# A two-layer hybrid decoder trunk: pre-norm row factors applied at the ends of the products, and the attention bias read from one small DRAM copy

## The chip, the cores and the metric

The kernel runs on one core of one Trainium2 chip. The time is device microseconds (us) of one execution. TensorE (PE) multiplies, VectorE (DVE), ScalarE (ACT) and GpSimd (POOL) do the rest, SyncE (SP) issues the loads of the weights. PE writes into PSUM; DVE and ACT read PSUM and SBUF. Each engine takes its instructions in the order of its own queue, and waits on semaphores where a value comes from another engine or from a DMA.

## The reference

The input `x` has 256 tokens (rows) of 1024 channels, in float32. There are two layers, each with FFN1, a mixer and FFN2; the mixer of layer 0 is an RG-LRU block, that of layer 1 is attention with one shared K and V, computed from the stream after layer 0.

```
def rms_norm(x, g):
    y = x * lax.rsqrt(jnp.mean(x * x, axis=-1, keepdims=True) + RMS_EPS)
    return y * g
def macaron_ffn(x, pre_g, post_g, w_gate, w_up, w_down):
    h = (silu(n @ w_gate) * (n @ w_up)) @ w_down          # n = rms_norm(x, pre_g)
    return x + 0.5 * rms_norm(h, post_g)
# layer:  x = macaron_ffn(x, ...); x = x + rms_norm(mixer(rms_norm(x, mix_pre_g)), mix_post_g)
#         x = macaron_ffn(x, ...)
# after layer 0:  k, v = split(rms_norm(x, kv_norm_g) @ w_kv)
# attention, one block of 256 keys:
#   s = q @ k.T * scale + rel_bias[h, t5_bucket(t - j)], -inf where j > t;  softmax(s) @ v
```

A pre-norm is thus a factor per row (token), `r = 1/sqrt(mean(x*x) + eps)`, and a gain per channel.

## The kernel before

Tokens lie in two tiles of 128 (`tt` 0 and 1), `x[tt]` stays in SBUF. Every float32 operand of a product is split into a high and a low float32r part, and a product is three PE products (`mm3`, L267 to L270): high by high, high by low, low by high. A weight piece of 2048 columns by 128 rows is loaded by SP into `raw`, and four instructions of ACT (`whi`, L273 or, with a channel's gain, L277) and four of DVE (`wlo`, L274 or L278) split it; three `raw` buffers and five pairs of `whi` and `wlo` are in flight. All weights, some 176 MB, pass through once.

Between two stages stands a **boundary**. When a token tile's last product has ended, `post` (L304) squares and sums it (ACT, `junk`), works out the post-norm's row factor (POOL, L288 and L289), and adds it to `x` (DVE, L313, two halves). Then `normed` (L317) does the same for the next stage's pre-norm: two squares on ACT, two sums on POOL, and `x` times the factor into `kb` (ACT L324 and DVE L325, half each). Then `turned` (L327) transposes `kb` on PE in eight 128x128 blocks (L336) and splits the result into `big`, the left or moving operand of the next stage. While tile 0 goes through this, PE still does products of tile 1; how many are left for it at that point is set in the code by where `turn_now` stands.

In the FFN the first four channel chunks are done token by token (`by_token`: gate and up for 128 tokens, `x` as the weights of PE); the later units channel by channel (`by_channel`, `wide`), where the result has channels on partitions and tokens along the free dimension. `dn` are the down products into `acc`. RG-LRU uses `yproj`, `yproj3` (by token), `xproj`, `yproj4` (by channel), `gates` and `scan`; attention uses `vals` (by token), `key` and `query` (by channel).

The attention bias: in FFN2 of layer 0 `bias_rows` makes 8 rows of 384 numbers, `bias_out` (L806) writes every row 128 times to DRAM, 8 x 128 x 384 x 4 bytes, in one DMA issued on ACT's queue, and in FFN1 of layer 1 `bias_tables` (L810) reads two tables of 128 x 4 x 256 back, with a step of 383 between partitions, so that each query row sees its row shifted by one.

The order of instructions on each engine is set when the kernel is built, by the order in the code with the weight splits at a lower priority (`Prog`).

Of the kernel before, what the change touches and what calls it, by code (L numbers as in the profile page):

```python
# [38 lines left out]
KB1 = 6  # L39
KB2 = 19  # L40
# [3 lines left out]
WIDE = True  # L44
# [42 lines left out]
def trunk_kernel(ctx, tc, t, out):  # L87
# [46 lines left out]
    make_identity(nc, ident)  # L134
    mhalf = cp.tile([P, 1], F32, tag="mhalf", name="mhalf")
# [149 lines left out]
    def rstd(ss, f):  # L285

        m, r = small(), small()
        nc.gpsimd.tensor_scalar(m, ss[:, 0:1], ss[:, 1:2], f * f * EPS, op0=ALU.add, op1=ALU.add)  # L288
        nc.gpsimd.tensor_tensor(r, m, mhalf, op=ALU.pow)  # L289
        return r  # L290
# [13 lines left out]
    def post(tt, src, g, half, out_rows=None):  # L304
# [6 lines left out]
        r = rstd(ss, f)  # L311
        for sl, y in zip(HALVES, ys):
            nc.vector.scalar_tensor_tensor(x[tt][:, sl], y, r, x[tt][:, sl], op0=ALU.mult, op1=ALU.add)  # L313
            if out_rows is not None:
                nc.sync.dma_start(out_rows[:, sl], x[tt][:, sl])

    def normed(tt, state):  # L317

        ss = small(2)
        for n, a in enumerate(halves(x[tt])):  # L320
            square_sum(a, 1.0, ss[:, n:n + 1])
        r = rstd(ss, 1.0)
# [4 lines left out]
    def turned(tt, state, g=None):  # L327
# [25 lines left out]
    def between(state, g, half=True):  # L353
# [12 lines left out]
    def ffn(which, l, state, after, nxt, middle={}, first=None):  # L366
# [40 lines left out]
        def by_channel(n):  # L407
# [3 lines left out]
            def wide(gi):  # L411
# [15 lines left out]
                if gi == 1:  # L427
# [8 lines left out]
            def go(gi):  # L436
                if WIDE:
                    return wide(gi)
                if gi == 0:
                    st["b", n] = bank().rearrange("p (g s) -> p g s", g=2)  # L440
                b = st["b", n]
                for k in range(KD):
                    wv = [a.rearrange("p (k g f) -> p k g f", k=4, g=2)[:, k % 4, gi, ft * P:(ft + 1) * P]
                          for a in pieces[keys(c)[k // 4]]]
                    mm3(b[:, gi, :], wv, xT(state, k), k == 0, k == KD - 1)
                if gi == 1:
                    sl, hd = kb1(), kb1()
                    nc.scalar.activation(sl, b[:, 0, :], AF.Silu)
                    nc.vector.tensor_mul(hd, b[:, 1, :], sl)
                    h = kb2(F32R, (P, 2, S))  # L450
                    split(h[:, 0, :], h[:, 1, :], hd)
                    for tt in range(NT):
                        hT[n, tt] = [h[:, part, tt * P:(tt + 1) * P] for part in range(2)]
            for gi in range(2):
                prog.add(lambda gi=gi: go(gi), *keys(c))
# [13 lines left out]

        def finish(units):  # L470
# [11 lines left out]
            prog.add(lambda: after(0, oacc[0], st["g"]))  # L482
# [9 lines left out]
            prog.add(lambda: after(1, oacc[1], st["g"]))  # L492

        if first is not None:
# [5 lines left out]
            tr(0, 0)  # L500
            by_channel(2)
# [29 lines left out]
        tr(1, 1)  # L531
        dn(3, 0)
# [35 lines left out]
    def recurrent(l, state, after, nxt):  # L568
# [10 lines left out]
        def yproj(tt, khs=(0, 1)):  # L579

            def use(b):
                st["sb", tt] = kb2()
                nc.scalar.activation(st["sb", tt], b, AF.Copy)
            by_token("lru_w_in", l, 2, tt, state, None, use, khs)

        def yproj3(tt):
# [3 lines left out]
            def go():  # L590
                b = bank()[:, 0:S]
                w = [a.rearrange("p (k f) -> p k f", k=8) for a in pieces[key]]
                for k in range(KD):
                    mm3(b, xT(state, k, tt), [a[:, k, :] for a in w], k == 0, k == KD - 1)
                st["sb3", tt] = kb1()
                nc.scalar.activation(st["sb3", tt], b, AF.Copy)
# [9 lines left out]
        def yproj4(n):  # L606

            def use(b):
                st["y4", n] = b
# [31 lines left out]
        def xproj(h, n):  # L641

            def use(b):
# [4 lines left out]
                nc.scalar.activation(cv[:, n, :], b, AF.Identity, scale=wcol[3], bias=cbias[:, 0, k:k + 1])  # L648
                for w in (2, 1, 0):
                    back = CW - 1 - w  # L650
                    nc.vector.scalar_tensor_tensor(cv[:, n, back:], b[:, 0:S - back], wcol[w],
# [97 lines left out]
        yproj3(1)  # L749
        xproj(0, 0)  # L750
# [42 lines left out]
    skew = {}  # L793

    def bias_rows():
# [6 lines left out]
        rr = skew["rows"] = big(shape=(P, Y))  # L802
# [3 lines left out]
    def bias_out():  # L806
        skew["dram"] = dp.tile([NH, P, Y], F32, tag="skew", name="skew")
        nc.scalar.dma_start(skew["dram"], skew["rows"][:NH, 0:Y].unsqueeze(1).to_broadcast([NH, P, Y]))

    def bias_tables():  # L810
        d = skew["dram"]
# [7 lines left out]
    def attention(j, l, state, kv_state, after, nxt):  # L819
# [7 lines left out]
        def vals(c, tt, khs=(0, 1)):  # L827
            def use(b):
                st["v", c, tt] = kb2()
                nc.scalar.activation(st["v", c, tt], b, AF.Copy)  # L830
            by_token("w_kv", None, 2 + c, tt, kv_state, ("kv_norm_g", 0), use, khs)

        def keep(what, h):
            def use(b):
                a = st[what, h] = kb2(F32R, (P, 2, S))
                split(a[:, 0, :], a[:, 1, :], b)
            return use

        def key(h):
            by_channel("w_kv", None, h // 2, h % 2, kv_state, ("kv_norm_g", 0), keep("k", h))  # L840
# [26 lines left out]
        def turned_p(h):  # L867
            def go():
# [3 lines left out]
                nc.tensor.transpose(pt[:, 0:P], p0[:, 0:P], ident)  # L872
                nc.tensor.transpose(pt[:, P:2 * P], p1[:, 0:P], ident)
                nc.tensor.transpose(pt[:, 2 * P:3 * P], p1[:, P:2 * P], ident)
# [100 lines left out]
    def begin():  # L975
        load_rows("first", (("ffn1_pre_g", 16),))
        normed(0, s1)
        turned(0, s1)
    begin()

    def second():
        load_x(1)
        with tc.issue_after(first_split[3].ins):
            normed(1, s1)
        s1["turn", 1] = lambda: turned(1, s1)
# [7 lines left out]
    def last(tt, src, g):  # L993
        post(tt, src, g, True, out.rearrange("b s d -> (b s) d")[tt * P:(tt + 1) * P, :])
# [3 lines left out]
    ffn(1, 1, s4, between(s5, ("mix_pre_g", 1)), s5, {9: bias_tables})  # L998
# [51 lines left out]
```

## Time and profile before

| | |
|---|---|
| median of 3 runs | 980.27 us (979.67 to 980.37) |
| the profiled execution | 980.36 us, span 978.5 us |
| PE busy | 943.1 us, 96% of the span |
| DVE, ACT, POOL busy | 69%, 64%, 3% |
| read from DRAM | 175.76 MB, 182 GB/s over the span with what is written |

The span goes from the first to the last instruction on the core. PE's busy time is modelled, and a busy PE need not be at its peak; idle time is what the trace shows between two of its instructions, with the event that ended it.

### The profile page before, as it was taken

Reading aid. Unit: us, or ns where it says so; the run is one execution under the profiler, and the core shown is the slowest. Engines: PE = TensorE matmul, PEld = TensorE weight load, DVE = VectorE, ACT = ScalarE, POOL = GpSimd, SP = SyncE. Lnnn points to the kernel's source line nnn. Section 1 sums busy time; section 2 is a strip of 40 time slices with the busy share of each in tenths; the row PEclk is TensorE's granted clock in tenths of the full one; section 3 lists DMA queues with packets and bytes.
Section 4 is the critical chain, followed back from the end, with each engine's and each line's share of the span. In section 5 each row is a group of like instructions: output and inputs, shape, how many; then the busy total and the mean of one; then the engine's idle time right before and its main releaser. Section 6 shows DMA issues by size and latency. Waiting matters only on the chain.

```text
span 978.5 us, 14039 instructions
## 1 busy us (share of the span) xinstructions
PE 943.1 (96%) x5124; PEld 808.6 (83%) x5124; DVE 675.5 (69%) x1332; ACT 631.1 (64%) x1325; POOL 26.8 (3%) x55
## 2 busy tenths in 40 slices
PE   6999999999989999599999999999999999999997
PEld 5888888879967888488878888887999878888886
DVE  5867775787888655385776767567987776757563
ACT  7757665678987655275775656567875675656562
POOL 1000000010010000000010000001000010000000
PEclk9999999999999999889999999999999999999999
DMA  8955656555157665676556656654735346656621
GB/s 258 327 170 186 202 188 221 166 175 194 49 171 261 201 207 118 162 231 200 160 187 235 208 179 192 196 193 153 236 130 176 126 129 237 203 185 184 203 86 44
DMA packets 131774, 179.29 MB, mean 183 GB/s; under 512 B 4689, under 2 KB 113401, under 8 KB 131705
## 3 DMA queue, kind: packets, MB, share of 16 engines
q1 hardware_dynamic: 129040, 175.65, 55.5%
q10 hardware_dynamic: 2664, 2.74, 1.9%
q8 instruction: 40, 0.66, 0.3%
q14 instruction: 30, 0.24, 0.1%
HBM read 175.76 MB, written 2.62 MB: 182 GB/s over the span
## 4 chain that ended last, share of the span: by engine, by line
issue 49%; PE 46%; POOL 2%; ACT 2%; DMA 1%; DVE 0%; SPq 0%; POOLq 0%; DVEq 0%; ACTq 0%
PE bank L421 7%; PE trb L421 7%; PE acc L268 4%; PE acc L269 4%; PE acc L270 4%; PE bank L268 3%; PE bank L269 3%; PE bank L270 3%; PE bank L420 3%; PE trb L420 3%; POOL small L288 1%; POOL small L289 1%; ACT junk L283 1%; DMA raw<-in_ffn_w_up_dram 1%; PE trb L423 0%
## 5 line engine op out<-in xcount | busy, mean ns | idle before, releaser
L278 DVE SCALAR_TENSOR_TENSOR wlo<-raw,cols,whi 128x512 fp32r<-128x512 f32 (+1 forms) x400 | 271.3, 726 | 66.2 <-ACT whi L277 66.1
L277 ACT ACTIVATE whi<-raw,cols 128x512 fp32r<-128x512 f32 (+1 forms) x400 | 255.9, 697 | 56.4 <-PE acc L270 27.3
L421 PE MATMUL bank<-big,whi 128*128 128x512 f32 x592 | 215.3, 398 | 0.0
L421 PE MATMUL trb<-big,whi 128*128 128x512 f32 x592 | 212.7, 394 | 0.0
L274 DVE TENSOR_TENSOR wlo<-raw,whi 128x512 fp32r<-128x512 f32 x264 | 170.7, 687 | 47.1 <-ACT whi L273 46.5
L268 PE MATMUL acc<-whi,kb 128*128 128x512 f32 x384 | 152.3, 397 | 10.4 <-ACT kb L273 10.4
L273 ACT ACTIVATE whi<-raw 128x512 fp32r<-128x512 f32 x264 | 151.0, 622 | 17.1 <-PE bank L269 8.2
L269 PE MATMUL acc<-wlo,kb 128*128 128x512 f32 x384 | 150.6, 392 | 0.0
L270 PE MATMUL acc<-whi,kb 128*128 128x512 f32 x384 | 149.7, 392 | 0.0
L420 PE MATMUL bank<-big,wlo 128*128 128x256 f32 x518 | 145.6, 281 | 0.0
L420 PE MATMUL trb<-big,wlo 128*128 128x256 f32 x518 | 143.4, 277 | 0.0
L421 PEld LDWEIGHTS bank<-big,whi 128*128 128x128 f32 x592 | 111.3, 188 | 23.6
L421 PEld LDWEIGHTS trb<-big,whi 128*128 128x128 f32 x592 | 111.0, 187 | 19.4
L420 PEld LDWEIGHTS bank<-big,wlo 128*128 128x128 f32 x518 | 98.1, 189 | 3.0
L420 PEld LDWEIGHTS trb<-big,wlo 128*128 128x128 f32 x518 | 97.3, 188 | 3.5
L268 PEld LDWEIGHTS acc<-whi,kb 128*128 128x128 f32 x384 | 72.6, 189 | 24.1 <-ACT kb L273 11.5
L270 PEld LDWEIGHTS acc<-whi,kb 128*128 128x128 f32 x384 | 72.6, 189 | 15.7
L269 PEld LDWEIGHTS acc<-wlo,kb 128*128 128x128 f32 x384 | 72.7, 189 | 14.9
L426 DVE TENSOR_TENSOR kb<-kb,trb 128x256 f32<-128x256 f32 x74 | 30.9, 418 | 76.1 <-ACT kb L425 76.0
L425 ACT ACTIVATE kb<-bank 128x256 f32<-128x256 f32 x74 | 28.5, 385 | 79.1 <-PE bank L421 79.1
L268 PE MATMUL bank<-whi,big 128*128 128x512 f32 (+1 forms) x176 | 70.4, 402 | 2.1 <-ACT big L273 1.4
L269 PE MATMUL bank<-wlo,big 128*128 128x512 f32 (+1 forms) x176 | 68.6, 393 | 0.0
(165 smaller groups left out, 1257.0 us busy)
## 6 DMA issues: line engine op xcount, KB each, us to landing
raw<-in_ffn_w_gate_dram SPq DMA_DIRECT2D x88, 512.0 KB, 4.1
raw<-in_ffn_w_up_dram SPq DMA_DIRECT2D x88, 512.0 KB, 5.1
raw<-in_ffn_w_down_dram SPq DMA_DIRECT2D x44, 1024.0 KB, 5.0
raw<-in_lru_w_in_dram SPq DMA_DIRECT2D x8, 1024.0 KB, 5.4
raw<-in_w_kv_dram SPq DMA_DIRECT2D x8, 1024.0 KB, 5.1
raw<-in_lru_w_out_dram SPq DMA_DIRECT2D x4, 1024.0 KB, 5.0
raw<-in_attn_w_q_dram SPq DMA_DIRECT2D x4, 1024.0 KB, 5.3
raw<-in_attn_w_o_dram SPq DMA_DIRECT2D x4, 1024.0 KB, 4.9
```

What stands on the lines that cost most here:

```text
L268: nc.tensor.matmul(o, a[0], b[0], start=start, stop=False)
L269: nc.tensor.matmul(o, a[0], b[1], start=False, stop=False)
L270: nc.tensor.matmul(o, a[1], b[0], start=False, stop=stop)
L273: nc.scalar.activation(hi, src, AF.Copy)
L274: nc.vector.tensor_sub(lo, src, hi.bitcast(F32))
L277: first_split.append(nc.scalar.activation(hi, src, AF.Copy, scale=g))
L278: nc.vector.scalar_tensor_tensor(lo, src, g, hi.bitcast(F32), op0=ALU.mult, op1=ALU.subtract)
L283: nc.scalar.activation(junk, a, AF.Square, scale=f / 32.0, accum_out=ss)
L420: nc.tensor.matmul(b[:, 1, :], wv[1], xt[:, 0, :], start=False, stop=False)
L421: nc.tensor.matmul(b, wv[0], xt, start=k == 0, stop=k == KD - 1)
L425: nc.scalar.activation(y, b[:, 1, :], AF.Copy)
L426: nc.vector.tensor_add(y, y, b[:, 0, :])
```

## The change

Row factors. Where a product's result has tokens on partitions, ACT's copy or Silu out of PSUM takes the factor as its scale; where it has tokens along the free dimension, DVE multiplies by a tile `R` of 128 x 256 that holds the factors of all tokens in every partition, made by `spread` once per stage. `turned` then transposes `x` itself; `factors` comes behind it. In an FFN only the gate is multiplied: the missing factor of the up product goes through to the post-norm, which removes it, with an epsilon made for it on POOL. The attention's queries keep the old way (`normed`), and are transposed by `flip`, a reversed identity, so that query rows run backwards and a bias table can be read with a step of 1 between partitions from one row per head.

```
-KB1 = 6
-KB2 = 19
+KB1 = 7
+KB2 = 17
+    flip = cp.tile([P, P], F32, tag="flip", name="flip")
...
+    def factors(tt, state):
+        ss = small(2)
+        for n, a in enumerate(halves(x[tt])):
+            square_sum(a, 1.0, ss[:, n:n + 1])
+        m = row("mean")
+        state["r", tt] = rstd(ss, EPS, m, row("factor"))
+        state["eps", tt] = row("eps")
+        nc.gpsimd.tensor_scalar(state["eps", tt], m, 4.0 * EPS, None, op0=ALU.mult)
+
+    def spread(state):
+        def go():
+            state["R"] = ws.tile([P, S], F32, tag="spread", name=nm("spread"), bufs=2)
+            pt = trb()
+            for tt in range(NT):
+                nc.tensor.transpose(pt[:, tt * P:(tt + 1) * P], state["r", tt].to_broadcast([P, P]), ident)
+            nc.vector.tensor_copy(state["R"], pt[:, 0:S])
+        prog.add(go)
...
+        src = state["xn", tt] if ("xn", tt) in state else halves(x[tt])
...
-                nc.tensor.transpose(pt[:, k * P:(k + 1) * P], state["xn", tt][h][:, k * P:(k + 1) * P], ident)
+                nc.tensor.transpose(pt[:, k * P:(k + 1) * P], src[h][:, k * P:(k + 1) * P],
+                                    ident if turn is None else turn)
...
-        def after(tt, src, post_g):
-            post(tt, src, post_g, half)
-            normed(tt, state)
-            state["turn", tt] = lambda: turned(tt, state, g)
+        def after(tt, src, post_g, eps=None):
+            post(tt, src, post_g, half, eps)
+            if turn is not None:
+                normed(tt, state)
+            def go():
+                turned(tt, state, g, turn)
+                if turn is None:
+                    factors(tt, state)
+            state["turn", tt] = go
...
-                        nc.scalar.activation(sl, b[:, 0:FC], AF.Silu)
+                        nc.scalar.activation(sl, b[:, 0:FC], AF.Silu, scale=state["r", tt])
...
+                if gi == 0:
+                    nc.vector.tensor_mul(y, y, state["R"])
+                else:
...
-                nc.scalar.activation(cv[:, n, :], b, AF.Identity, scale=wcol[3], bias=cbias[:, 0, k:k + 1])
+                xb = kb1()
+                nc.vector.tensor_mul(xb, b, state["R"])
+                nc.scalar.activation(cv[:, n, :], xb, AF.Identity, scale=wcol[3], bias=cbias[:, 0, k:k + 1])
...
-        skew["dram"] = dp.tile([NH, P, Y], F32, tag="skew", name="skew")
-        nc.scalar.dma_start(skew["dram"], skew["rows"][:NH, 0:Y].unsqueeze(1).to_broadcast([NH, P, Y]))
+        bias["dram"] = dp.tile([NH, Y], F32, tag="bias", name="bias")
+        nc.scalar.dma_start(bias["dram"], bias["rows"][:NH, 0:Y])
...
-            src = bass.AP(tensor=d.tensor, offset=d.offset + 127 + 4 * q * P * Y,
-                          ap=[[Y - 1, P], [P * Y, 4], [1, S]])
+            src = bass.AP(tensor=d.tensor, offset=d.offset + 4 * q * Y, ap=[[1, P], [Y, 4], [1, S]])
...
-                nc.tensor.transpose(pt[:, 0:P], p0[:, 0:P], ident)
+                nc.tensor.transpose(pt[:, 0:P], p0[:, 0:P], flip)
```

`yproj4` and `key` get the same multiplication by `R` as `xproj`; `yproj`, `yproj3` and `vals` get the factor as the scale of their copies. Over the whole program DVE gains 92 multiplications of 128x256 (74 in the FFNs, 10 in RG-LRU, 8 keys) and 5 copies of `spread`, and loses 10 of its 12 L325; ACT loses 10 of its 12 L324; PE gains 10 transposes; POOL gains 10 small products for the epsilons.

The order on PE where RG-LRU hands over to FFN2 of layer 0. `acc` with the higher number is the second half of tile 1's output product, `trb` takes the transposes, and `bank` is FFN2's first product. Before:

```order
L268 MATMUL acc_2798<-whi_2813,big_2793 128x512
L269 MATMUL acc_2798<-wlo_2814,big_2793 128x512
L270 MATMUL acc_2798<-whi_2813,big_2793 128x512
L336 MATMUL trb_2926<-ident,kb_405_2888 128x128 x4
L336 MATMUL trb_2935<-ident,kb_406_2889 128x128 x4
L268 MATMUL bank_2995<-whi_2838,big_2922 128x512
```

The same place on PE in the changed kernel:

```order
L366 MATMUL trb_2960<-ident,x_67 128x128 x4
L366 MATMUL trb_2969<-ident,x_67 128x128 x4
L272 MATMUL acc_2844<-whi_2860,big_2840 128x512
L273 MATMUL acc_2844<-wlo_2861,big_2840 128x512
L274 MATMUL acc_2844<-whi_2860,big_2840 128x512
L272 MATMUL acc_2845<-whi_2860,big_2840 128x512
L273 MATMUL acc_2845<-wlo_2861,big_2840 128x512
L274 MATMUL acc_2845<-whi_2860,big_2840 128x512
L272 MATMUL bank_3027<-whi_2885,big_2956 128x512
```

The transposes of tile 0 read `x` and stand ahead of the last six products of tile 1's output, not behind them.

The order on DVE at that place in the changed kernel, from tile 1's output (`acc_2844`, `acc_2845`) on. `big` are the splits of tile 0, `x_165` is tile 1 of the stream, and `wlo_3018` is the low part of the second weight piece of FFN2:

```order
L771 TENSOR_TENSOR kb_422_2995<-acc_2844,bout_1977 128x512
L771 TENSOR_TENSOR kb_423_2996<-acc_2845,bout_1977 128x512
L278 TENSOR_TENSOR big_2957<-trb_2960,big_2957 128x2x128
L278 TENSOR_TENSOR big_2958<-trb_2969,big_2958 128x2x128
L315 TENSOR_TENSOR kb_425_3000<-kb_422_2995,gain_1975 128x512
L315 TENSOR_TENSOR kb_426_3001<-kb_423_2996,gain_1975 128x512
L278 TENSOR_TENSOR big_2959<-trb_2969,big_2959 128x2x128
L318 SCALAR_TENSOR_TENSOR x_165<-kb_425_3000,small_3009,x_165 128x512
L318 SCALAR_TENSOR_TENSOR x_165<-kb_426_3001,small_3009,x_165 128x512
L282 SCALAR_TENSOR_TENSOR wlo_3018<-raw_3014,cols_904,whi_3017 128x512 x2
```

Both updates of tile 1's `x` stand ahead of the second weight piece's low part, as they do in the kernel before (`x_162` ahead of `wlo_2986`); the multiplication of tile 0 (L325) is gone.

## Rows read from the trace of the kernel before

**Rows 1.** PE's waits over the span: for whom, total, times, longest.

```profile
PE acc L268 <- ACT kb L273: 10.4, 1, 10.4
PE trb L336 <- ACT kb L324: 10.2, 7, 2.8
```

**Rows 2.** Windows: length, busy PE, PEld, DVE, ACT, POOL, granted clock, DMA share, GB/s.

```profile
405.50:416.00 10.50, 0.13 (x1) 0.13 (x1) 3.98 (x8) 4.00 (x9) 0.00 (x0) 0.62 0.78 234
416.00:422.00 6.00, 6.00 (x16) 4.74 (x17) 4.81 (x9) 4.97 (x11) 0.00 (x0) 0.52 0.79 242
288.80:292.00 3.20, 3.18 (x8) 2.50 (x9) 2.35 (x6) 2.83 (x7) 1.07 (x2) 0.50 0.51 177
```

**Rows 3.** Timeline of ACT in FFN2 of layer 0: start, length, [idle before, releaser].

```profile
373.15 0.79 ACTq L808 DMA_DIRECT2D skew<-big  x1
...
410.75 1.33 ACT L277 ACTIVATE whi<-raw,cols 128x512 fp32r<-128x512 f32 x2 [15.67 <-DMA raw<-in_ffn_w_up_dram]
```

**Rows 4.** DMA view, 383 to 393 us in 40 slices; then issues, KB, us to landing.

```profile
DMA  4444444444444444446364454545554877699998
GB/s 49 49 43 49 49 49 49 49 49 49 49 49 49 49 49 70 109 135 147 100 164 119 152 158 129 158 125 152 174 180 164 207 225 188 182 258 256 238 233 184
...
gain<-in_ffn_post_g_dram SPq DMA_DIRECT2D x4, 512.0 KB, 6.5
...
big<-skew ACTq DMA_DIRECT2D x2, 512.0 KB, 3.7
```

**Rows 5.** Timeline of PE: the transposes at the boundaries and their waits.

```profile
198.17 1.09 PE L336 MATMUL trb<-ident,kb 128*128 128x128 f32 x8 [1.24 <-ACT kb L324]
...
287.33 1.09 PE L336 MATMUL trb<-ident,kb 128*128 128x128 f32 x8 [2.81 <-ACT kb L324]
...
296.60 0.55 PE L336 MATMUL trb<-ident,kb 128*128 128x128 f32 x3 [0.48 <-ACT kb L324]
...
492.35 1.09 PE L336 MATMUL trb<-ident,kb 128*128 128x128 f32 x8 [1.42 <-ACT kb L324]
...
784.82 1.09 PE L336 MATMUL trb<-ident,kb 128*128 128x128 f32 x8 [0.72 <-ACT kb L324]
```

**Rows 6.** Timeline where RG-LRU hands over to FFN2.

```profile
282.31 1.42 DVE L313 SCALAR_TENSOR_TENSOR x<-kb,small,x 128x512 f32<-128x512 f32 x2 [0.84 <-POOL small L289]
...
286.56 0.72 ACT L324 ACTIVATE kb<-x,small 128x512 f32<-128x512 f32 x1 [0.53 <-POOL small L289]
...
286.96 1.28 DVE L740 TENSOR_TENSOR kb<-acc,bout 128x512 f32<-128x512 f32 x2
...
292.00 0.74 DVE L313 SCALAR_TENSOR_TENSOR x<-kb,small,x 128x512 f32<-128x512 f32 x1
...
292.66 0.75 DVE L278 SCALAR_TENSOR_TENSOR wlo<-raw,cols,whi 128x512 fp32r<-128x512 f32 x1
...
294.46 0.50 PE L269 MATMUL bank<-wlo,big 128*128 128x512 f32 x1
```

**Rows 7.** Timeline of the start, ACT and PE.

```profile
8.65 1.33 ACT L277 ACTIVATE whi<-raw,cols 128x512 fp32r<-128x512 f32 x2 [1.00 <-DMA raw<-in_ffn_w_up_dram]
...
10.30 0.80 PE L268 MATMUL bank<-whi,big 128*128 128x512 f32 x1 [0.63 <-ACT big L273]
```

**Rows 8.** Groups by form: count, busy us, mean ns, idle before.

```profile
L426 DVE TENSOR_TENSOR kb<-kb,bank 128x256 f32<-128x256 f32 x74 | 31.0, 418 | 41.3 <-ACT kb L425 41.2
...
L325 DVE TENSOR_SCALAR kb<-x,small 128x512 f32<-128x512 f32 x12 | 5.8, 486 | 12.9 <-POOL small L289 12.9
```

**Rows 9.** Windows in RG-LRU and at the start of attention, columns as in rows 2.

```profile
250.00:275.00 25.00, 24.33 (x150) 21.27 (x149) 24.15 (x43) 24.27 (x44) 0.00 (x0) 1.00 0.26 85
...
675.00:700.00 25.00, 23.76 (x142) 20.79 (x141) 23.06 (x52) 22.89 (x61) 3.48 (x7) 1.00 0.60 196
```

**Rows 10.** Timeline of ACT in one channel unit of FFN2.

```profile
369.57 0.42 ACT L429 ACTIVATE kb<-kb 128x256 f32<-128x256 f32 x1 [0.61 <-DVE kb L426]
...
371.49 0.36 ACT L425 ACTIVATE kb<-trb 128x256 f32<-128x256 f32 x1
```

More of the change, by code (lines that the diff above doesn't have):

```diff
@@ L134, in trunk_kernel @@
     make_identity(nc, ident)
+    flip = cp.tile([P, P], F32, tag="flip", name="flip")
+    nc.gpsimd.memset(flip, 0.0)
+    nc.gpsimd.affine_select(out=flip, in_=flip, pattern=[[1, P]], compare_op=ALU.not_equal, fill=1.0,
+                            base=-(P - 1), channel_multiplier=1)
     mhalf = cp.tile([P, 1], F32, tag="mhalf", name="mhalf")
@@ L310, in post @@
             nc.vector.tensor_mul(ys[n], src[n], g[:, HALVES[n]])
-        r = rstd(ss, f)
+        r = rstd(ss, f * f * EPS if eps is None else eps)
         for sl, y in zip(HALVES, ys):
@@ L325, in normed, with row, turned @@
         nc.vector.tensor_scalar(state["xn", tt][1], x[tt][:, HALVES[1]], r, None, op0=ALU.mult)
-    def turned(tt, state, g=None):
+    def row(tag):
+        return ws.tile([P, 1], F32, tag=tag, name=nm(tag), bufs=6)
+    def factors(tt, state):
[14 more added lines that the diff above has]
+        prog.add(go)
+    def turned(tt, state, g=None, turn=None):
         if "x" not in state:
             state["x"] = [big(F32R, (P, 2, 2, S)) for _ in range(KD // 2)]
+        src = state["xn", tt] if ("xn", tt) in state else halves(x[tt])
         tok = slice(tt * P, (tt + 1) * P)
@@ L434, in wide @@
                         hT[n, tt] = [h[:, part, tt * P:(tt + 1) * P] for part in range(2)]
[L436 to L453, printed above, removed]
             for gi in range(2):
-                prog.add(lambda gi=gi: go(gi), *keys(c))
+                prog.add(lambda gi=gi: wide(gi), *keys(c))
         NF = FF // P
@@ L468, in dn, with end @@
             prog.add(go, key)
+        def end(tt):
+            prog.add(lambda: after(tt, oacc[tt], st["g"], state["eps", tt]))
         def finish(units):
@@ L481, in finish @@
             dn(NF - 1, 0)
-            prog.add(lambda: after(0, oacc[0], st["g"]))
+            end(0)
             if nxt is None:
@@ L491, in finish @@
                 dn(NF - 1, 1)
-            prog.add(lambda: after(1, oacc[1], st["g"]))
+            end(1)
         if first is not None:
@@ L500, in ffn @@
             tr(0, 0)
+            spread(state)
             by_channel(2)
@@ L531, in ffn @@
         tr(1, 1)
+        spread(state)
         dn(3, 0)
@@ L582, in use @@
                 st["sb", tt] = kb2()
-                nc.scalar.activation(st["sb", tt], b, AF.Copy)
+                nc.scalar.activation(st["sb", tt], b, AF.Copy, scale=state["r", tt])
             by_token("lru_w_in", l, 2, tt, state, None, use, khs)
@@ L595, in go @@
                 st["sb3", tt] = kb1()
-                nc.scalar.activation(st["sb3", tt], b, AF.Copy)
+                nc.scalar.activation(st["sb3", tt], b, AF.Copy, scale=state["r", tt])
             prog.add(go, key)
@@ L749, in recurrent @@
         yproj3(1)
+        spread(state)
         xproj(0, 0)
@@ L792, in trunk_kernel @@
     dp = ctx.enter_context(tc.tile_pool(name="dp", bufs=1, space=bass.MemoryType.DRAM))
-    skew = {}
+    bias = {}
     def bias_rows():
@@ L801, in bias_rows @@
         nc.tensor.matmul(b[:NH, 0:Y], rb[:NB, 0:NH], oh[:NB, 0:Y], start=True, stop=True)
-        rr = skew["rows"] = big(shape=(P, Y))
+        rr = bias["rows"] = big(shape=(P, Y))
         nc.vector.memset(rr[:NH, S:], NEG)
@@ L829, in use, with keep @@
                 st["v", c, tt] = kb2()
-                nc.scalar.activation(st["v", c, tt], b, AF.Copy)
+                nc.scalar.activation(st["v", c, tt], b, AF.Copy, scale=kv_state["r", tt])
             by_token("w_kv", None, 2 + c, tt, kv_state, ("kv_norm_g", 0), use, khs)
-        def keep(what, h):
+        def keep(what, h, by=None):
             def use(b):
                 a = st[what, h] = kb2(F32R, (P, 2, S))
+                if by is not None:
+                    y = kb1()
+                    nc.vector.tensor_mul(y, b, by["R"])
+                    b = y
                 split(a[:, 0, :], a[:, 1, :], b)
@@ L976, in begin @@
         load_rows("first", (("ffn1_pre_g", 16),))
-        normed(0, s1)
         turned(0, s1)
+        factors(0, s1)
     begin()
@@ L982, in second, with go @@
         load_x(1)
-        with tc.issue_after(first_split[3].ins):
-            normed(1, s1)
-        s1["turn", 1] = lambda: turned(1, s1)
+        def go():
+            turned(1, s1)
+            factors(1, s1)
+        s1["turn", 1] = go
     def later():
@@ L991, in later, with last @@
         lru_consts()
-    def last(tt, src, g):
-        post(tt, src, g, True, out.rearrange("b s d -> (b s) d")[tt * P:(tt + 1) * P, :])
+    def last(tt, src, g, eps):
+        post(tt, src, g, True, eps, out.rearrange("b s d -> (b s) d")[tt * P:(tt + 1) * P, :])
     ffn(1, 0, s1, between(s2, ("mix_pre_g", 0)), s2, {9: later}, second)
@@ L997, in trunk_kernel @@
     ffn(2, 0, s3, between(s4, None), s4, {9: bias_rows, 11: bias_out})
-    ffn(1, 1, s4, between(s5, ("mix_pre_g", 1)), s5, {9: bias_tables})
+    ffn(1, 1, s4, between(s5, ("mix_pre_g", 1), turn=flip), s5, {9: bias_tables})
     attention(0, 1, s5, s4, between(s6, None, half=False), s6)
```

27 lines of the change are left out of this document (13 added, 14 removed).

## The prediction

> **What bounds the kernel now.** The table of busy times comes first: PE is busy 943.1 of 978.5 us, so only time that PE loses can be won, and work added to DVE or ACT is free until PE waits for it. The next view is the list of PE's waits [rows 1]. It shows one wait of 10.4 us, for ACT's split of a hidden unit (L273), and seven waits of 10.2 us in all for the normalised rows of `kb` (L324). Everything else that PE waits for is below 1.5 us, apart from the first 5 us of the program.
>
> The windows show what an idle stretch costs beyond itself. After the long wait PE runs at a granted clock of 0.52 (the lower of its two levels, 1.2 of 2.4 GHz) for 6.00 us, and after a wait of 2.81 us at 0.50 for 3.20 us [rows 2, 5]; after the waits of 1.24 and 1.42 us no such window shows.
>
> The timeline of ACT tells what the 10.4 us are. ACT stood 15.67 us for a gate and up piece of the weights, and 37 us ahead of that it had issued the write of the bias copies, 8 x 128 x 384 x 4 = 1.57 MB [rows 3]. In the DMA view, while nothing but that write runs, the engines are 0.4 busy and move 49 GB/s; a load arriving beside it gets little more than 150 GB/s [rows 4]. PE lived from finished pieces until 405.5 us, then stood. So the write is slow, sits on the same DMA engines as the weights, and is the cause of the long wait.
>
> **The change, part by part.** All terms are against the profiled execution's own 980.36 us, which lies 0.09 us above the median of 980.27, so the two are one number here.
>
> The bias write shrinks from 1.57 MB to 12 KB. The wait of 10.40 us goes, and the slow clock behind it: 6.00 us at 0.52 hold 3.1 us of work at full clock, so 2.9 go too [rows 1, 2]. Nothing else late stands behind it, since DVE and ACT were busy only 4 of the 10.5 us of the stall itself. Term: **-13.3**, at least -10.4 if part of the slow stretch comes back elsewhere. The table's read keeps its 1 KB runs and 128 partitions; only the addresses now overlap. No row shows just this read. The nearest are the same-sized read, landed in 3.7 us, and the gain loads, where 128 partitions read one 4 KB row, in 6.5 us per 512 KB [rows 4]. At 6.5 us each, some 190 us ahead of its first use, it costs nothing; the bad end is the write's pace (a rival below).
>
> The boundaries. For tile 0 the steps from `x` to `kb` go off PE's path: at RG-LRU's end `x` is there at 283.73 and `kb`'s copy starts at 286.56 [rows 6], so nearly 3 us come off a chain that PE waits for by 1.24, 2.81, 1.42 and 0.72 us [rows 5]. Five waits of that kind are removed; the boundary into attention keeps `normed`, and its wait. Besides, the transposes now stand ahead of six products, 1.4 us of cover for the splits. For the entries of RG-LRU, of FFN1 of layer 1 and of the last FFN2 I take the idle time: -1.24, -1.42, -0.72, together **-3.4**. The lower bound is nothing, if the splits of ACT and DVE are late instead; the upper is some 2 us more, as later waits for splits shrink as well.
>
> The entry of FFN2 of layer 0 is another matter. PE ends tile 1's output at 287.33 - 2.81 = 284.5, with the eight transposes (1.09) inside now at 285.6, and could go on at once. But the second weight piece's low part stands behind both updates of tile 1 on DVE, as the order shows. From L740 to the second L313's end that chain took 292.74 - 286.96 = 5.8 us [rows 6]; started at 285.6 it ends at 291.4, the first low part comes 0.75 us later, at 292.1. The product that needs it started at 294.46: won 2.3 us, not the 4 that the front of the queue promises. Meanwhile PE has only 12 products of the first piece, 2.7 us, and then stands some 3 us. That is as long as the wait that brought the clock down to 0.50 [rows 2], and I charge 0.8 of the 1.6 us which that stretch lost, since DVE paces PE there anyway. The wait of 0.48 at 296.60 goes. Term: -2.3 + 0.8 - 0.5 = **-2.0**, between 0 and -5.3 (all of 2.81, 1.6, 0.48 and 0.4 of splits).
>
> The Trainium skill ("TensorE: Matmul & The Clock Gate", Part 1) says that the slow clock is the default and activity releases it; by that rule the new stand of 3 us brings it in full, which would make this term -1.2, and the trace so far agrees, with 0.50 after 2.81 us.
>
> The start. The first product waits for the split of `x`, which stands behind two splits of weights of 0.67 us; now it stands behind one [rows 7]. Term **-0.6**, from nothing to -1.3.
>
> What is added. `spread` puts 10 transposes on PE; eight took 1.09 us at a boundary [rows 5], so **+1.4**. The 92 multiplications on DVE are of the shape of L426, 0.418 us [rows 8]: 38.5 us, less 10 x 0.486 for L325. In an FFN unit the multiplication sits between the gate's sum and the Silu. The Silu started at 369.57, and its unit's up product was only copied out at 371.49 [rows 10], nearly 2 us of slack for 0.42; the unit's `dn` comes a whole unit later. So 74 of them are hidden by PE's own products; without that cover they are 31 us. The other 18 lie where DVE has less to spare: 24.15 of 25 us at RG-LRU's scan and 23.06 of 25 at attention's start [rows 9]. Of 18 x 0.42 = 7.6 us, two in the former window and some five in the latter meet a full DVE, 2.9 us; PE lost only 1.9 us in both windows together, so it has cover, and I take **+0.5**, from nothing to 2.9. The copies with a scale, the epsilons and the smaller pool of buffers I take at nothing: POOL is 3% busy, and the pool of `kb` loses two buffers but also the four that held `kb` at each boundary.
>
> Sum: 980.36 - 13.3 - 3.4 - 2.0 - 0.6 + 1.4 + 0.5 = **963.0 us**, 1.8% less.
>
> **The rivals.**
> *The splits are the limit.* If at the boundaries ACT and DVE, both above 0.8 busy there, take as long as before, the waits only change their names: no -3.4 and -2.0, 968.4. For it: the order of DVE at FFN2's entry. Against it: ACT and DVE idled in the very chain that is removed.
> *All of it arrives.* The boundary terms reach their upper ends, -5.4 and -5.3, the start -1.3: 957.0.
> *The read crawls as the write did.* 1.05 MB of overlapping reads against 1.57 MB of writes: 2/3 of 13.3 comes back, 971.9. Against it: the gain loads at 6.5 us.
> *The write was not the cause.* The stall stays: 976.3. Against it: nothing else ran at 383 us.
> *Slower: the FFN multiplications come into the path.* If DVE, with one more instruction in each unit, delivers the Silu's input too late, 74 x 0.42 = 31 us come on top: 994. The kernel turns slower once 0.23 us (17.4/74) of each multiplication shows in PE's time. Against it: the 2 us of slack.
>
> **How the numbers follow.** Chances: the forecast's case 0.58, all of it arrives 0.14, the splits are the limit 0.17, the read crawls 0.03, the write is not the cause 0.03, the multiplications in the path 0.05. The first three lie between 955 and 969, and that is the range: it holds nearly 0.9 by this list, and I leave it so, as the terms at the boundaries can miss by more than their bounds. A difference below 0.2% can't be told from none here, so: faster 0.95, same 0.01, slower 0.04; of the multiplications' case a fifth stays faster.
>
> **What the profile after would show.** The wait for L273 gone from PE's list, and no granted clock near 0.5 around 400 us: right about the write. A read of `bias` that lands within 7 us: right about the read. No PE wait on a transpose at three boundaries, but PE standing about 3 us near FFN2's entry for `x`, or for `wlo`, with a slow clock behind it: right about the order. PE waits inside the channel units of any FFN, or a wait of Silu that ends after the up product's end: the slower case. The prediction is wrong if the weights now come late elsewhere, or if DVE at the scan makes PE stand for more than 3 us.

## The result, and the profile after

The changed kernel takes 963.82 us (median of 4 runs, 963.35 to 964.19), the kernel before 979.97 on the same chip: a ratio of 0.9833, 95% interval 0.9821 to 0.9845. The forecast was 963.0. The profiled execution took 963.35 us, its span is 961.3, so it is compared with the 978.5 of before. Line numbers below are those of the kernel that a row comes from; in the changed one L318 is the update of `x`, L366 a boundary's transposes, L329 the normalised row, L352 the transposes of `spread`, L466 the new multiplication of an FFN unit.

PE's waits (for whom, total, times, longest):

```profile
PE trb L164 <- DMA rows<-in_ffn_pre_g_dram: 5.0, 1, 5.0
PE bank L272 <- ACT big L277: 2.4, 1, 2.4
PE trb L366 <- DVE x L318: 1.6, 1, 1.6
PE trb L366 <- ACT kb L329: 1.2, 1, 1.2
PE acc L272 <- ACT big L277: 1.0, 2, 0.5
PE trb L352 <- POOL factor L293: 0.9, 1, 0.9
PE bank L273 <- DVE wlo L282: 0.9, 2, 0.6
```

The wait of 10.4 us for the split of a hidden unit is gone, and of the seven waits for normalised rows, 10.2 us in all [rows 1], one of 1.2 is left, at the entry of attention, which keeps `normed`. Three waits are new: 1.6 us for `x`, 0.9 us for POOL's factor, and two together of 0.9 us for low parts of weights.

The windows (columns as in rows 2) cover RG-LRU's end and FFN2's entry, and the stretch in which the long stall stood:

```profile
284.00:292.00 8.00, 6.40 (x30) 4.44 (x29) 7.51 (x15) 6.83 (x18) 3.31 (x5) 1.00 0.45 137
292.00:300.00 8.00, 7.07 (x30) 4.75 (x30) 7.81 (x16) 5.97 (x14) 0.74 (x2) 1.00 0.46 145
...
400.00:422.00 22.00, 22.00 (x118) 18.80 (x117) 16.44 (x32) 14.16 (x29) 0.00 (x0) 1.00 0.57 179
```

PE is busy in all 22 us where it had stood 10.4 and run 6.00 at a granted clock of 0.52, the lower of the two levels (1.2 of 2.4 GHz) [rows 2]; at FFN2's entry no window shows a clock under 1.00. The timeline of PE, from which the units below are read too:

```profile
9.61 0.79 PE L272 MATMUL bank<-whi,big 128*128 128x512 f32 x1 [2.44 <-ACT big L277]
...
24.94 0.32 PE L352 MATMUL trb<-ident,factor 128*128 128x128 f32 x1 [0.94 <-POOL factor L293]
...
196.66 1.03 PE L366 MATMUL trb<-ident,x 128*128 128x128 f32 x8
...
282.75 1.30 PE L366 MATMUL trb<-ident,x 128*128 128x128 f32 x8
...
288.28 0.63 PE L272 MATMUL bank<-whi,big 128*128 128x512 f32 x2
290.47 1.29 PE L366 MATMUL trb<-ident,x 128*128 128x128 f32 x8 [1.56 <-DVE x L318]
291.70 0.50 PE L273 MATMUL bank<-wlo,big 128*128 128x512 f32 x1
...
474.39 1.03 PE L366 MATMUL trb<-ident,x 128*128 128x128 f32 x8
...
767.26 1.03 PE L366 MATMUL trb<-ident,x 128*128 128x128 f32 x8
...
801.93 0.39 PE L459 MATMUL bank<-big,whi 128*128 128x512 f32 x1
...
938.26 0.40 PE L459 MATMUL bank<-big,whi 128*128 128x512 f32 x1
```

The transposes of tile 0 at 196.66, 282.75, 474.39 and 767.26 begin without a wait, where those of rows 5 waited 1.24, 2.81, 1.42 and 0.72 us. Tile 1's transposes, at 290.47, waited for the second update of `x` on DVE; the product behind them, at 291.70, needs the low part of the second weight piece, which DVE made after that update:

```profile
285.57 1.29 DVE L771 TENSOR_TENSOR kb<-acc,bout 128x512 f32<-128x512 f32 x2
...
289.57 1.42 DVE L318 SCALAR_TENSOR_TENSOR x<-kb,small,x 128x512 f32<-128x512 f32 x2 [0.49 <-POOL small L293]
290.90 1.41 DVE L282 SCALAR_TENSOR_TENSOR wlo<-raw,cols,whi 128x512 fp32r<-128x512 f32 x2
```

The bias read, seen in the DMA view of 476 to 496 us as the queue of ACT's transfers (packets, MB, share of 16 engines):

```profile
q10 hardware_dynamic: 1056, 1.05, 15.5%
```

These are 15.5% of 20 us, 3.1 us of all the engines for 1.05 MB: reads whose addresses overlap do not crawl, and no engine waited for them. From issue to landing the DMA view gives 4.4 us for the same read in the one copy below, within the 7 us that the prediction named.

**Where the time went, by stretches.** In every FFN at least 18 channel units follow each other (FFN1 of layer 0 has 20, and its first two count with the start), and but for the long stall PE doesn't wait in them. Their first and last gate products cut the span into stretches that can be compared from kernel to kernel (us; the first and the last start of each FFN from the timeline of PE; three of the kernels are those of the experiments below):

| stretch | before | one copy | normed back | after | both, places |
|---|---|---|---|---|---|
| start to first unit | 44.56 | 44.31 | 46.43 | 44.77 | 44.90 |
| units, FFN1 layer 0 | 136.03 | 136.03 | 136.41 | 136.41 | 136.03 |
| RG-LRU with both entries | 143.29 | 143.36 | 144.56 | 140.51 | 140.42 |
| units, FFN2 layer 0 | 150.28 | 136.91 | 137.32 | 137.32 | 136.91 |
| into FFN1 layer 1 | 51.69 | 51.63 | 51.74 | 49.82 | 49.78 |
| units, FFN1 layer 1 | 135.94 | 135.95 | 136.32 | 136.32 | 135.95 |
| attention with both entries | 158.05 | 158.07 | 158.40 | 156.78 | 155.92 |
| units, FFN2 layer 1 | 135.88 | 135.95 | 136.33 | 136.33 | 135.94 |
| last unit and end | 22.81 | 22.81 | 23.01 | 23.00 | 22.91 |
| span | 978.53 | 965.02 | 970.52 | 961.26 | 958.76 |

### The profile page after: what moved, and what is told of

Read it like the earlier page. It is cut to its first block, busy times and chain, and to the rows that moved or that the text cites. A ratio compares the mean times of both kernels' runs of the same rounds, so it can differ in the third digit from the quotient of the medians.

```text
span 961.3 us, 14151 instructions
## 1 busy us (share of the span) xinstructions
PE 940.9 (98%) x5134; PEld 806.4 (84%) x5134; DVE 710.7 (74%) x1419; ACT 625.3 (65%) x1315; POOL 35.1 (4%) x67
## 4 chain that ended last, share of the span: by engine, by line
PE 72%; issue 20%; DVE 3%; ACT 3%; DMA 1%; POOL 1%; SPq 0%; POOLq 0%; DVEq 0%; ACTq 0%
PE trb L459 11%; PE bank L459 11%; PE acc L274 7%; PE acc L272 7%; PE acc L273 7%; PE bank L273 5%; PE bank L272 5%; PE bank L274 5%; PE trb L458 5%; PE bank L458 5%; DMA raw<-in_ffn_w_up_dram 1%; PE bank L461 1%; PE trb L461 1%; PE trb L366 1%; ACT junk L287 1%
## 5 line engine op out<-in xcount | busy, mean ns | idle before, releaser
L459 PE MATMUL trb<-big,whi 128*128 128x512 f32 x592 | 215.2, 398 | 0.0
L459 PE MATMUL bank<-big,whi 128*128 128x512 f32 x592 | 212.9, 395 | 0.0
L278 DVE TENSOR_TENSOR wlo<-raw,whi 128x512 fp32r<-128x512 f32 x264 | 173.6, 688 | 33.8 <-ACT whi L277 29.5
L277 ACT ACTIVATE whi<-raw 128x512 fp32r<-128x512 f32 x264 | 153.2, 623 | 43.8 <-PE trb L459 28.9
L458 PE MATMUL trb<-big,wlo 128*128 128x256 f32 x518 | 145.5, 281 | 0.0
L458 PE MATMUL bank<-big,wlo 128*128 128x256 f32 x518 | 143.4, 277 | 0.0
L272 PE MATMUL bank<-whi,big 128*128 128x512 f32 (+1 forms) x176 | 68.4, 393 | 3.3 <-ACT big L277 2.4
```

The source lines that it names most:

```text
L272: nc.tensor.matmul(o, a[0], b[0], start=start, stop=False)
L277: nc.scalar.activation(hi, src, AF.Copy)
L278: nc.vector.tensor_sub(lo, src, hi.bitcast(F32))
L458: nc.tensor.matmul(b[:, 1, :], wv[1], xt[:, 0, :], start=False, stop=False)
L459: nc.tensor.matmul(b, wv[0], xt, start=k == 0, stop=k == KD - 1)
```

## The experiments

Each ratio is to the kernel before, run on the same chip; that of the change is 0.9833.

**One copy.** The kernel before with the bias edit alone (and one 2 KB buffer less, for room):

```
-        nc.scalar.dma_start(skew["dram"], skew["rows"][:NH, 0:Y].unsqueeze(1).to_broadcast([NH, P, Y]))
+        nc.scalar.dma_start(bias["dram"], bias["rows"][:NH, 0:Y])
...
-KB2 = 19
+KB2 = 18
```

> The kernel before with only the bias edit (8 rows written once, tables read with a step of 1, queries and probabilities turned by the reversed identity; one buffer of the 2 KB pool less, for room). Theory: the slow write alone made the long stall, 10.4 us of idle PE and 2.9 of slow clock, so 980.1 - 13.3 = 966.8 us, between 966 and 968, with PE's wait for ACT's split near 405 us gone and the boundary waits of up to 2.8 us still there. Rival, the row factors free ACT and DVE and the write is innocent: 976 to 980 us, the stall still there.

Measured 966.86 us, ratio 0.9864 (0.9850 to 0.9877). Its list of PE's waits begins with the boundaries; the split of the hidden unit is not in it:

```profile
PE trb L340 <- ACT kb L328: 10.1, 7, 2.8
```

The table puts the gain where the stall was: the units of FFN2 take 136.91 in place of 150.28, 13.37 us less, and no other stretch moves by more than 0.25. The write made the stall, and no other stretch shows it.

**Rows only.** The changed kernel with the old write, the old orientation of the queries and the old read.

```
-        nc.scalar.dma_start(bias["dram"], bias["rows"][:NH, 0:Y])
+        nc.scalar.dma_start(skew["dram"], skew["rows"][:NH, 0:Y].unsqueeze(1).to_broadcast([NH, P, Y]))
```

> The changed kernel with the old bias write of 1.57 MB and the old orientation of the queries. Theory: the stall comes back whole, 963.8 + 13.3 = 977.1 us, between 976 and 978.5; row factors are worth about 3 us. Rival, the row factors took the stall away: 964 to 967 us.

Measured 974.52 us, ratio 0.9942 (0.9928 to 0.9955). The stall is back, but smaller. PE's long wait in the kernel before, then the same here:

```profile
415.87 0.80 PE L268 MATMUL acc<-whi,kb 128*128 128x512 f32 x1 [10.40 <-ACT kb L273]
```

```profile
413.19 0.79 PE L272 MATMUL acc<-whi,kb 128*128 128x512 f32 x1 [7.70 <-ACT kb L277]
```

The write and ACT's wait for the weights here:

```profile
371.24 0.79 ACTq L840 DMA_DIRECT2D skew<-big  x1
...
409.05 1.33 ACT L281 ACTIVATE whi<-raw,cols 128x512 fp32r<-128x512 f32 x2 [13.04 <-DMA raw<-in_ffn_w_up_dram]
```

So 977.1 was wrong by 2.6 us. The units of FFN2 take 148.56 here, 11.24 above those of the changed kernel and not 13.37: the same write, issued 1.9 us earlier than in the kernel before, held the weights up for 13.04 us where it had been 15.67 [rows 3]. PE ran dry at the same time in both, at 405.47 (415.87 - 10.40) and 405.49 (413.19 - 7.70), so the earlier write let PE go on earlier, by 2.68 us. Why PE lasted as long here, though its units had begun 1.36 us earlier (322.52 against 323.88), was not settled. It follows that the two parts don't simply add: alone the row factors are worth some 6 us, on top of the bias edit 3.

**Write from 128 partitions.** The kernel before; the rows are made 16 times over, on 128 partitions, and the same 1.57 MB are written from there.

```
+        nc.vector.tensor_copy(rb16[:NB, 0:P].rearrange("b (h r) -> b h r", h=NH),
+                              rb[:NB, 0:NH].unsqueeze(2).to_broadcast([NB, NH, P // NH]))
...
-        nc.scalar.dma_start(skew["dram"], skew["rows"][:NH, 0:Y].unsqueeze(1).to_broadcast([NH, P, Y]))
+        nc.scalar.dma_start(skew["dram"].rearrange("h (r c) y -> (h r) c y", c=NH),
+                            skew["rows"][:, 0:Y].unsqueeze(1).to_broadcast([P, NH, Y]))
```

> The kernel before; the same 1.57 MB go to DRAM, but the 8 rows stand 16 times on 128 partitions and each partition writes 8 copies. Theory of pace (the write from 8 partitions kept 0.4 of the engines at 49 GB/s): from 128 partitions it takes 4 to 13 us, the weights are late by less than PE's 37 us of pieces in hand, and the stall goes: 966.5 to 969 us. Rival, the amount of bytes beside the weights: 972 to 980 us, with the stall for the split of the hidden unit still several us.

Measured 966.62 us, ratio 0.9861 (0.9848 to 0.9875): as good as the single copy. The write's queue in the DMA view, first in the kernel before (373 to 415 us), then here (373 to 383 us):

```profile
q10 hardware_dynamic: 1032, 1.57, 33.5%
```

```profile
q10 hardware_dynamic: 1040, 1.57, 48.2%
```

Before, a packet took 0.335 x 42 x 16 / 1032 = 0.218 us, here 0.482 x 10 x 16 / 1040 = 0.074 us. With as many bytes and nearly as many packets the write is over within 10 us, where PE in the kernel before ran dry only 32 us after the issue (373.15 to 405.47). So the pace stalled the kernel, not the amount. The pace had two parts: fewer engines at work, as their share of 0.4 in rows 4 shows, and each packet three times as long. By the trace's records of DMA packets, never more than 8 of the write's are under way at once in the 33 us that it lasts in the kernel before, and up to 19 in its 7.7 us here. The Trainium skill ("DMA: Bandwidth & Descriptors", Rules for kernel authors) says that an outermost dimension of fewer than 16 confines a transfer to at most that many engines; with 8 rows outermost, the trace agrees with its 8 packets at most and its 0.4 of 16 engines. Why a packet took three times as long no run shows.

**Normed back.** The changed kernel with normalised rows at every boundary, and factors of one, so that all that was added stays.

```
+    ones = cp.tile([P, 1], F32, tag="ones", name="ones")
+    nc.gpsimd.memset(ones, 1.0)
+    eps4 = cp.tile([P, 1], F32, tag="eps4", name="eps4")
+    nc.gpsimd.memset(eps4, 4.0 * EPS)
...
-            if turn is not None:
-                normed(tt, state)
+            normed(tt, state)
+            state["r", tt], state["eps", tt] = ones, eps4
             def go():
                 turned(tt, state, g, turn)
-                if turn is None:
-                    factors(tt, state)
```

> The changed kernel with the normalised rows made before the transposes again at the five boundaries that had lost them, and factors of one in the copies, multiplications and spreads, so that all added instructions stay. Theory: only the waits at the boundaries come back, with the sizes of the kernel before: 963.8 + 1.2 + 3.7 + 1.4 + 0.7 = 970.8 us, at least 969 (the terms of the forecast, 5.4). Rival, the waits only changed their names and the row factors gained nothing there: 963.5 to 965.5 us.

Measured 971.20 us, ratio 0.9910 (0.9896 to 0.9923). The waits stand again where they stood [rows 5]:

```profile
200.68 1.09 PE L370 MATMUL trb<-ident,kb 128*128 128x128 f32 x8 [1.25 <-ACT kb L333]
...
290.96 1.09 PE L370 MATMUL trb<-ident,kb 128*128 128x128 f32 x8 [2.61 <-ACT kb L333]
...
482.65 1.09 PE L370 MATMUL trb<-ident,kb 128*128 128x128 f32 x8 [1.46 <-ACT kb L333]
...
775.83 1.09 PE L370 MATMUL trb<-ident,kb 128*128 128x128 f32 x8 [0.67 <-ACT kb L333]
...
789.47 0.41 PE L440 MATMUL trb<-ident,kb 128*128 128x128 f32 x2 [0.72 <-DVE big L282]
```

The last of these lines is a wait behind the boundary, for the transposes of a hidden unit (0.61 us in the kernel before); the changed kernel has none there. The slow clock behind the longest wait is back too (columns as in rows 2):

```profile
292.80:296.40 3.60, 3.60 (x10) 2.82 (x9) 2.75 (x7) 3.23 (x10) 1.07 (x2) 0.53 0.38 130
```

In the table the three stretches with boundaries are 4.05, 1.92 and 1.62 us longer than in the changed kernel, 7.59 together: that is what the boundaries gained. The profiled execution was the slowest of this kernel's (972.3 us, the others 970.95 to 971.20); its start, 46.43, is 1.66 later than in the changed kernel, so the medians (7.4 us apart) rather than the spans (9.2) go with the 7.59. Against the one copy the same stretches are 1.20, 0.11 and 0.33 longer, 1.64 us: the price of what was added in them.

**No multiplication, and four.** The changed kernel without the FFNs' multiplications by `R` (the gate of the channel units lacks its factor), and with three more, by one.

```
-                    nc.vector.tensor_mul(y, y, state["R"])
```

```
                     nc.vector.tensor_mul(y, y, state["R"])
+                    nc.vector.tensor_mul(y, y, ones.to_broadcast([P, S]))
+                    nc.vector.tensor_mul(y, y, ones.to_broadcast([P, S]))
+                    nc.vector.tensor_mul(y, y, ones.to_broadcast([P, S]))
```

> The changed kernel without the 74 multiplications by the row factors in the channel units of the FFNs (the gate is left without its factor). The FFNs' products ran some 2 us longer than before over the four FFNs with no wait that the list shows, about 0.03 us for each multiplication. Theory: the cover of 2 us hides the multiplications but for this drift, so 963.8 - 2 = 961.8 us if the drift is theirs, 963.8 if it is not. Rival, the multiplications stand in the path: 963.8 - 31 = 933 us.

> The changed kernel with three more multiplications, by one, behind each of the 74 in the channel units. Theory, all of them fit in the 2 us before the up product's copy (4 x 0.42 = 1.7): 964 to 966 us if DVE's use is free, 963.8 + 3 x 2 = 970 us if each one costs the drift of 0.03 us. Rival, the cover is smaller than it looked: 963.8 + 3 x 31 = 1057 us at most, anything above 975 speaks for it.

Measured 963.71 us without (0.9833, 0.9819 to 0.9846) and 963.88 us with four (0.9835, 0.9821 to 0.9848), against 963.82 with one. One window of 18 us in FFN2 of layer 1, of the changed kernel and of that with four:

```profile
829.00:847.00 18.00, 18.00 (x98) 15.40 (x97) 13.18 (x25) 11.19 (x23) 0.00 (x0) 1.00 0.55 176
```

```profile
829.00:847.00 18.00, 18.00 (x98) 15.41 (x97) 15.41 (x31) 11.34 (x23) 0.00 (x0) 1.00 0.52 176
```

DVE works 2.2 us more, PE is busy throughout in both. The 17 units between the first and the last start of that FFN take 136.3 us without the multiplications and with four, as with one. The multiplications are hidden four times over, and the drift of 0.02 us a unit is not theirs: the expectation that laid it to them was wrong.

**Queries too.** The attention's queries without normalised rows as well: `x` turned by `flip`, and a reversed `R` multiplied on.

```
-            if turn is not None:
-                normed(tt, state)
...
-                if turn is None:
-                    factors(tt, state)
+                factors(tt, state)
...
-            by_channel("attn_w_q", j, h // 2, h % 2, state, None, keep("q", h))
+            by_channel("attn_w_q", j, h // 2, h % 2, state, None, keep("q", h, state))
...
+        spread(state, flip)
```

> The changed kernel with the queries treated like the rest: x itself turned by the reversed identity, the queries multiplied by a reversed spread of the factors (8 multiplications and 2 transposes more, 2 normalised rows less). Theory: the wait of 1.23 us at the entry of attention goes, +0.3 for the transposes, so 962.9 us, 962.2 to 963.8. Rival, DVE is full there (23.5 of 25 us) and the 8 multiplications of 0.42 us show: 965 to 967 us.

Measured 963.47 us, 0.9832 (0.9818 to 0.9845), no difference that the times can tell. The wait of 1.2 us for L329 is gone from PE's list; a wait of 0.4 us at L352 came, and the attention stretch is 156.15 in place of 156.78, so half of the wait was gained, by one execution of each.

**Spread late.** The first `spread` behind the gate products of the first channel unit.

```
+                if "R" not in state:
+                    spread(state, now=True)
                 y = st["y", n, gi] = kb1()
...
             tr(0, 0)
-            spread(state)
             by_channel(2)
```

> The changed kernel with the first spread's transposes behind the eight gate products of the first channel unit instead of ahead of them. Theory: PE's wait of 0.94 us for POOL's factor near 25 us goes, 962.9 us, 962.5 to 963.4. Rival, the time is then lost at the next wait there (the unit's sum waits for the spread): 963.8 us.

Measured 962.69 us, 0.9823 (0.9809 to 0.9836), as the theory said, 1.1 us less; the 0.9 us for POOL's factor are gone from the list, and the first unit of the table starts at 43.77.

**Pools, and the turn of the PSUM buffers.** The remaining question was why a channel unit lasts 8.019 us ((938.26 - 801.93) / 17) where it lasted 7.997 in the one copy ((942.21 - 806.26) / 17). The one copy with the new buffer counts (its edit stands here against the one copy), and the changed kernel with one `trb` buffer skipped at each spread:

```
-KB1 = 6
-KB2 = 18
+KB1 = 7
+KB2 = 17
```

```
+            trb()
             pt = trb()
```

> The kernel before with the bias edit and the buffer counts of the change (7 of 1 KB, 17 of 2 KB). A channel unit of the FFNs lasts 7.997 us in the kernel before and 8.019 in the changed one, with or without the multiplications. Theory: the buffer counts, by the addresses that they give, make the difference: 8.019 us a unit, and 966.9 + 72 x 0.022 = 968.4 us. Rival, the turn of the two PSUM buffers of the transposes, which the spread shifts by one: units of 7.997, 966.9 us.

> The changed kernel, in which each spread skips one of the two PSUM buffers of the transposes, so that the up products take the buffers that they had before. Theory of the buffers' turn: units of 7.997 us again, 963.8 - 1.6 = 962.2 us. Rival, the buffer counts in SBUF: units stay at 8.019, 963.8 us.

Measured 967.64 us (0.9874, 0.9860 to 0.9887) and 963.41 us (0.9833, 0.9820 to 0.9847). The units tell more than the times: 7.997 us in the first (135.95 in 17 units), 8.019 in the second (136.32). Both theories fall.

**Both, and places.** First the two edits together, then the same with one tile of each pool asked for ahead of the others, in the order in which the kernel before asks. Places in SBUF are given when the kernel is built, in the order of the first demand: the kernel before first demands what `normed` needs, the changed one first demands `big`.

```
     def begin():
+        small(2), kb1(), small(), kb2(), big()
         load_rows("first", (("ffn1_pre_g", 16),))
```

> The queries without normalised rows and the first spread behind its gate products, together. Theory: the two gains add, 963.8 - 0.35 - 1.1 = 962.4 us, 961.8 to 962.8, faster than both kernels. Rival, they lean on the same slack: 962.7 us as for the late spread alone.

> The last kernel (queries without normalised rows, first spread late) with one buffer of each pool asked for ahead of the rest, in the order of the kernel before: the tiles then lie in SBUF where they lay before (the moving operand big from 176864 on in place of 134112). Neither buffer counts, nor the turn of PSUM buffers, nor the multiplications made the channel unit 8.019 us in place of 7.997. Theory of places: with the operands where they were, units of 7.997 us, 961.8 - 1.6 = 960.2 us, 959.8 to 960.8. Rival, something else that came with the row factors: 8.019 us and 961.8 us.

Measured 961.78 us (0.9819, 0.9805 to 0.9832) and 960.01 us (0.9796, 0.9782 to 0.9809). The first is 0.6 us below the sum of the two gains and at the lower end of what was expected, the second as the theory of places said. The first and last unit of the last FFN, in the first and in the second kernel:

```profile
800.62 0.39 PE L456 MATMUL bank<-big,whi 128*128 128x512 f32 x1
...
936.95 0.40 PE L456 MATMUL bank<-big,whi 128*128 128x512 f32 x1
```

```profile
799.91 0.39 PE L456 MATMUL bank<-big,whi 128*128 128x512 f32 x1
...
935.85 0.39 PE L456 MATMUL bank<-big,whi 128*128 128x512 f32 x1
```

136.33 and 135.94 us: 8.019 us a unit, and 7.996 once the tiles lie where they lay. The instructions of every engine and their order are the same in both kernels. Where the 0.4 us lie can be read from the starts of the products in the timeline of PE, summed over the 17 units: from the first kernel to the second the gate products go from 47.24 to 47.82 us, the up products from 47.90 to 47.24, the down products from 40.96 to 40.66. Gate and up, which read `big`, nearly cancel; 0.30 us come from the down products, which read hidden units and weights and not `big`. This kernel beats both that the study began with, by some 4 us the changed one.

## Why the prediction was right, and where only its sum was

The total was met within 0.8 us, but partly by luck: the boundaries gave 2.2 us more than forecast, and the start, the units and the end together took 2.6 us more. By the stretches, against the span of before:

| term | forecast | measured | from |
|---|---|---|---|
| bias write | -13.3 | -13.4 | one copy, units of FFN2 |
| boundaries (-3.4 and -2.0) | -5.4 | -7.6 | normed back less after |
| transposes, 18 multiplications | +1.9 | +1.7 | 7.59 less the 5.92 that the three stretches won (8 of the 10 transposes lie in them) |
| start | -0.6 | +0.2 | 44.56 to 44.77 |
| units of the FFNs | 0 | +1.6 | 4 stretches, 150.28 taken as 136.91 |
| end | 0 | +0.2 | 22.81 to 23.00 |
| sum | -17.4 | -17.3 | |

*The write.* Right in place, cause and size, and shown by the one copy. It was the pace, as the prediction read from the 49 GB/s, and the same bytes at another pace cost nothing. The read is fast, also as forecast. One reading of rows 4 was off, though nothing rests on it: beside the write's 49 GB/s the sum reaches 258, so a load got up to some 210 GB/s and not little more than 150.

*The boundaries.* The mechanism was right: the waits on `kb` vanished, and normed back brought them back with 7.59 us, so the rival in which waits only change their names falls. The size was too small by 2.2 us. In the stretch of RG-LRU 4.05 us were won for a forecast of 3.2 (1.24 and 2.0); the missing 0.8 is the slow clock that was charged and did not come, as told below. In the attention stretch 0.72 was forecast and 1.62 won: the forecast counted the idle time ahead of the transposes and left the waits behind them to its bound, and there the 0.72 us at 789.47 went as well. In the stretch into FFN1 of layer 1 the forecast was 1.42 and 1.92 were won; where the other half microsecond lay was not traced.

*FFN2's entry.* The order on DVE worked as told: from the start of L771 to the end of `x` 290.99 - 285.57 = 5.4 us (forecast 5.8, ending at 291.4), and the product with the first low part came at 291.70 (forecast 292.1). What failed is the stand of 3 us and the 0.8 us for the slow clock behind it. PE had two more products to do, until 288.91, waited 1.56 us and then did tile 1's transposes until the low part was there. Two shorter waits for low parts followed, 0.3 and 0.6 us. The granted clock stayed at 1.00 after 1.56 us without work, as after the 1.24 and 1.42 of rows 5. A stand of 3 us did not come, so what it would have cost is not shown; the 2.61 us in normed back did bring the lower clock.

*The start.* The first product began at 9.61 in place of 10.30, 0.69 earlier (forecast 0.6). The step that failed is what was left out behind it: the first `spread` waits for POOL's factor of tile 1, 0.94 us. Spread late took that back. The start also scatters from one execution to the next, so the 0.2 is no firm number. Over the seven kernels with the first `spread` in its early place the first product began at 9.27 to 10.27 and the first unit of the table at 44.77 to 46.43; over the four kernels without row factors they began at 10.07 to 10.78 and at 44.31 to 45.24. By the means the first product came 0.7 us earlier, about as forecast, and the unit 0.9 us later. The changed kernel's profiled execution was its fastest, and the medians lie 16.2 us apart where the spans differ by 17.3.

*The multiplications.* The 74 are hidden, and with four times as many they still are: the rival on the other side was further off than its 0.05 said. The other 18 lie within the 1.7 us.

*The units.* "The smaller pool of buffers I take at nothing" was right about the counts and missed the places: 0.4 us in each FFN came from where the tiles lie in SBUF, by the new order of first demand. Shown is that the places do it (three other causes were tried and fell), and that the down products bear most of it; not which operand's place, nor by what mechanism. The edit also moves the turn of the buffers in each pool by one, which was not tried alone.

*The end.* Of the 0.2 us one half is the slower products: PE ended 16.75 us behind the last unit's start, where it had been 16.63, and 16.63 again with the old places. The rest is POOL's sum with the epsilon of its own, 0.37 us in place of 0.30; the epsilons had been taken at nothing.

## What to carry to other kernels

Price a stall by the stretch that holds it, and ask of a slow transfer whether its amount or its shape makes the pace: 1.57 MB from 8 partitions cost 13.4 us, from 128 partitions nothing that the times can tell. When a value is moved to a later place, look for the first consumer that is now early: here the first `spread` waited 0.94 us for what nothing had needed so soon. And when a phase without waits changes its length by a fraction of a per cent, compare where the tiles lie before blaming the added instructions.

## What the runs showed of the hardware that was not expected

The places of tiles in SBUF change the speed of PE with the same instructions: 8.019 against 7.997 us for a unit, 0.4 us in each of the four FFNs and 1.6 us of the whole; most of it, 0.30 of 0.38 us in one FFN, is in the down products. A write from 8 partitions takes 0.218 us for a packet of 1.5 KB, one from 128 partitions 0.074. Reads with a step of one element between partitions cost about what those with a step of 383 do: 3.1 us of all engines, against 17.8% of 20 us or 3.6 for the read of before, and 4.4 us to landing (in the one copy) against 3.7.
